# A two-sequence encoder on one core: norm_w applied to the tokens instead of the projection weights, each weight chunk split in one operation per engine

## The chip, the core and the metric

One core of a Trainium2 chip runs the whole program. Its engines are TensorE (PE in the rows, with PEld for its weight loads), VectorE (DVE), ScalarE (ACT), GpSimd (POOL) and SyncE (SP), which issues most transfers. The metric is the device time of one execution in microseconds.

## The reference

A trunk of two layers, D_MODEL 1024, runs over two token sequences, x_prompt of 512 tokens and x_sample of 1024, with the same weights. Cut to what matters:

```
h = rms_norm(x, norm_w[l])            # x * rsqrt(mean(x*x) + EPS) * norm_w
proj = h @ w_in[l]                    # 1024 -> 3328 columns
q, k, v, g_a, u_h, g_h = split(proj)
attn = gqa_attention(rope(rms_norm(q)), rope(rms_norm(k)), v)     # 8 query heads, 2 key heads
o_a = rms_norm(attn, attn_out_norm_w[l]) * silu(g_a)
v_h, x1, x2 = split(short_conv(u_h))
zz = x1 * long_conv(v_h, filter 0);  zz = x2 * long_conv(zz, filter 1)
o_h = rms_norm(zz, hyena_out_norm_w[l]) * silu(g_h)
x = x + concat([o_a, o_h]) @ w_out[l]
...
y = rms_norm(x, final_norm_w)
```

norm_w may be multiplied into h or into the rows of w_in; the product is the same.

## The kernel before

Tokens are handled in tiles of 128 and blocks of 512: block 0 is the short sequence (tiles 0 to 3), blocks 1 and 2 the long one (tiles 4 to 11). Every operand of a large product is kept as two f16 halves, a high one and a low one, and a product is three matmuls (high x high, high x low, low x high). A split into halves is therefore always a pair: ACT writes the high half (a copy with a scale), and DVE writes what is left (scalar_tensor_tensor: in * scale - high).

The weights w_in come in chunks of 256 columns for all 1024 rows, laid out as 128 partitions x 8 row groups x 256 columns (2048 f32 a partition). There are 13 chunks a layer. `w_chunk` (L545) loads one, splits it with eight pairs, one for each row group k, because the scale is norm_w of that group's rows, a column of 128 values (`par_s`, L408 makes it with the factor S_W), and keeps the halves in DRAM for the other sequence; 26 chunks in all are split so. `norm_T` (L484) takes one token tile x with its root r, splits x * r into halves by one pair of 1024 columns, and transposes both halves by a DMA on SP's queue (L492) into hT, the operand of all projections. It is called for four tiles at a time in `first_norm` (L500, layer 0: blocks 1, 2, then 0) and for two tiles at a time in `out` (L1242, layer 1).

Shorthands record nearly every instruction: `act` is L308, `stt` L320, `tt` L328, `ts` L334, `red` L340, `mm` L346, so rows of the profile carry those lines and are told apart by shape.

The work is written as three threads (L45), each a list of parts with a letter, the layer and the sequence (0 short, 1 long): n norm, q queries, keys, values and gates, u convolution inputs and gates, e and f filters, t attention, c long convolutions, a and o the two halves of the output projection. So c10 is the convolution of layer 1 for the short sequence and o11 the last output projection of the long one. `emit` (L353) takes one step at a time from a thread, so that two counters keep a ratio: `dve` grows with every `stt`, `tt` and `red` on DVE (65 + 1.04 per column, L312), `tens` with every matmul (L344). By turns it prefers a part that loads PE or one that loads DVE. A convolution's channel tile c may start only when the part u of its sequence has marked that half as done (L748, L1021). Buffers come from one arena by age. A scheduler then sets each engine's order from the priorities of emission; matmuls of the projections are put 100 places back (PX).

Of the kernel before, what the change touches and what calls it, by code (L numbers as in the profile page):

```python
# [14 lines left out]
ALU = mybir.AluOpType  # L15
# [32 lines left out]
# column offsets of the per-channel parameters  # L48
C_NW, C_CW, C_CB, C_DEC, C_HB, C_AW, C_HW, C_N = 0, 8, 44, 56, 72, 80, 84, 88

S_H = 2.0 ** 10      # normalised activations
S_W = 2.0 ** 8       # projection weights
S_QK = 2.0 ** 7      # q and k after rotation
S_V = 2.0 ** 8
S_P = 2.0 ** 14      # softmax weights
S_C = 2.0 ** 11      # transform matrices
S_F = 2.0 ** 13      # filters
S_OA = 2.0 ** 8      # gated attention output
S_OH = 2.0 ** 10     # gated hyena output
S_U = (2.0 ** 6, 2.0 ** 8)   # folded conv inputs  # L60
S_Y = (2.0 ** 5, 2.0 ** 7)   # spectra of conv outputs
# [11 lines left out]
def _tables():  # L73
# [31 lines left out]
    for L in (LA, LB):  # L105
# [12 lines left out]
        "t_t": np.ascontiguousarray(np.concatenate(ts)[None, :]),  # L118
    }
# [22 lines left out]
class Arena:  # L142
    """On-chip memory in units of 1 KB a partition. A piece is taken that has been free for a while, small
    short-lived ones from the low end and the others from the high end; if there is none, the piece that has
    been free for longest."""
# [41 lines left out]
class Psum:  # L187
    """PSUM banks by class of use; in each class the banks free for longest are taken first."""
# [29 lines left out]
class Thread:  # L218
    """Parts of the work in their order, as steps."""
# [14 lines left out]
class Kern:  # L234
# [24 lines left out]
    def share(self, name, load):  # L259
        """Buffers that several threads read: loaded by the first, freed by the last."""  # L260
        if name not in self.shared:
            self.shared[name] = [load(), 0]
        self.shared[name][1] += 1
        return self.shared[name][0]
# [10 lines left out]
    def keep(self, n):  # L275
        """Columns that stay."""
        o = self.small_n
        self.small_n += n
        assert self.small_n <= 512
        return self.small[:, o:o + n]  # L280

    def tmp(self, n):
        """Columns that are soon used up."""
# [12 lines left out]
    def early(self, ap):  # L296
        """Instructions that free a PSUM bank go before others of their time."""
# [55 lines left out]
    def emit(self, threads):  # L353
        """Emit threads side by side, so that the work of VectorE keeps to RATIO times that of TensorE: by
        turns one whose present part loads TensorE more, or one whose present part loads VectorE more."""
# [31 lines left out]
    def rsqrt(self, out, ss, n, a, b):  # L387
        """out = (a * ss + b) ** -0.5 on [P, n] columns."""
# [11 lines left out]
    def prologue(self):  # L400
# [4 lines left out]
        for l in range(DEPTH):  # L405
            par = self.cols[:, l * C_N:(l + 1) * C_N]
            ps = self.keep(C_N)
            self.ts(ps[:, C_NW:C_NW + 8], par[:, C_NW:C_NW + 8], S_W)  # L408
# [6 lines left out]
            self.par_s.append(ps)  # L415

    def sine(self, out, x, n):
        """out = sin(x) with x taken into [-pi, pi]."""
# [13 lines left out]
    def features(self):  # L432
        """Hidden layers of the filter networks, one layer of the trunk in each half of the partitions;
        each is stored as a stack of a high and a low half."""
# [49 lines left out]
    def norm_T(self, l, x, t, r):  # L484
        m = self.m
        hb = m.alloc(4)
        hl = hb.f16().rearrange("p (h d) -> p h d", h=2)
        self.act(hl[:, 0], x, AF.Copy, scale=r)
        self.stt(hl[:, 1], x, r, hl[:, 0], ALU.mult, ALU.subtract)
# [863 lines left out]
```

## Time and profile before

| | us |
|---|---|
| median of 3 runs | 2420.97 |
| lowest, highest | 2419.26, 2422.30 |
| span of the profiled execution | 2406.2 |
| PE busy | 2061.8 |
| DVE busy | 1853.7 |
| ACT busy | 1146.9 |
| POOL busy | 432.0 |

The span runs from the first to the last instruction of the profiled execution, whose own time outside the span is not listed; the median of the runs is 14.8 us above its span. An engine's busy time is the union of its instructions. Since the engines run side by side, the busy times add up to far more than the span.

### The profile page before, as it was taken

The numbers are of one execution on the slowest core, as the hardware profiler recorded it, in microseconds if no ns is written. First come the engines' busy times: TensorE is split into PE (matmuls) and PEld (weight loads), VectorE is DVE, ScalarE is ACT, GpSimd is POOL, SyncE is SP. The second block draws the span as 40 slices with busy tenths as digits, with TensorE's granted clock in tenths as the row PEclk, the third lists the DMA queues.
The fourth block names the chain that finished last, engine by engine and source line by source line (L and its number), as shares of the span: only waits on it lengthen the run. The fifth ranks groups of instructions, "written<-read, shape, count | busy, mean of one in ns | idle before, by whom it ended". The sixth has DMA issues, their size and how long they took to land. (4 is left out here: it accounts for less than half of the span.)

```text
span 2406.2 us, 39740 instructions
## 1 busy us (share of the span) xinstructions
PE 2061.8 (86%) x15436; PEld 1249.0 (52%) x15436; DVE 1853.7 (77%) x3109; ACT 1146.9 (48%) x2016; POOL 432.0 (18%) x288
## 2 busy tenths in 40 slices
PE   5888889999989889878798778899999998887587
PEld 3656544444554556555575645444446445555453
DVE  7777677777767889976778767687777776998966
ACT  6545445766644234223544445366655652232322
POOL 1323120000110222222223312100011002222321
PEclk9899999999999899989899989999999999999789
DMA  8686659989999668688956678688989999574664
GB/s 230 151 209 174 166 152 216 225 187 203 230 253 265 189 171 215 193 260 266 222 137 191 169 184 215 177 195 192 225 187 197 225 264 305 173 202 118 204 203 136
DMA packets 774534, 485.86 MB, mean 202 GB/s; under 512 B 664838, under 2 KB 720295, under 8 KB 761288
## 3 DMA queue, kind: packets, MB, share of 16 engines
q1 hardware_dynamic: 773952, 482.96, 78.6%
q8 instruction: 121, 1.98, 0.3%
q14 instruction: 69, 0.57, 0.1%
q10 hardware_dynamic: 392, 0.34, 0.1%
HBM read 192.76 MB, written 139.20 MB: 138 GB/s over the span
## 5 line engine op out<-in xcount | busy, mean ns | idle before, releaser
L346 PE MATMUL psum<-arena 128*128 128x512 f16 (+4 forms) x15052 | 2018.5, 300 | 311.7 <-DMA arena<-arena 150.8
L346 PEld LDWEIGHTS <-arena 128*128 128x128 f16 (+2 forms) x15040 | 1199.0, 104 | 1087.5 <-issue 450.4
L328 POOL TENSOR_TENSOR arena<-arena 128x512 f32<-128x512 f32 (+4 forms) x218 | 415.2, 1912 | 1750.7 <-ACT arena L308 1032.4
L328 DVE TENSOR_TENSOR arena<-arena 128x1024 f32<-128x1024 f32 (+4 forms) x484 | 524.5, 1114 | 68.0 <-POOL arena L328 26.9
L308 ACT ACTIVATE arena<-arena 128x512 f16<-128x512 f32 (+4 forms) x359 | 265.1, 753 | 386.3 <-DVE arena L328 208.2
L320 DVE SCALAR_TENSOR_TENSOR arena<-arena,ring 128x1024 f16<-128x1024 f32 (+2 forms) x292 | 352.7, 1224 | 62.7 <-ACT arena L308 61.4
L308 ACT ACTIVATE arena<-psum 128x512 f32<-128x512 f32 (+2 forms) x336 | 177.2, 533 | 386.7 <-PE psum L346 380.6
L308 ACT ACTIVATE arena<-arena,ring 128x1024 f16<-128x1024 f32 (+1 forms) x280 | 287.2, 1044 | 148.9 <-DVE ring L939 29.8
L340 DVE TENSOR_REDUCE ring<-psum 128x1 f32<-128x1024 f32 (+1 forms) x192 | 197.5, 1039 | 55.6 <-PE psum L346 55.4
L308 ACT ACTIVATE arena<-arena,small 128x256 f16<-128x256 f32 (+5 forms) x288 | 167.2, 628 | 143.5 <-DMA arena<-in_p_win_dram 27.0
L320 DVE SCALAR_TENSOR_TENSOR arena<-psum,small,arena 128x511 f32<-128x511 f32 (+2 forms) x240 | 173.4, 743 | 63.8 <-PE psum L346 42.0
L320 DVE SCALAR_TENSOR_TENSOR arena<-psum,arena 128x512 f32<-128x512 f32 (+2 forms) x188 | 107.4, 598 | 129.7 <-ACT arena L308 121.0
L308 ACT ACTIVATE arena<-psum,ring 128x1024 f32<-128x1024 f32 (+1 forms) x192 | 185.6, 967 | 5.0 <-DMA g<-arena 0.5
L320 DVE SCALAR_TENSOR_TENSOR arena<-arena,small 128x256 f16<-128x256 f32 (+1 forms) x224 | 123.5, 583 | 22.9 <-ACT arena L308 15.2
L320 DVE SCALAR_TENSOR_TENSOR arena<-arena 128x512 f32<-128x512 f32 (+5 forms) x135 | 119.4, 890 | 11.7 <-ACT arena L308 11.1
L320 DVE SCALAR_TENSOR_TENSOR arena<-arena,psum 128x512 f32<-128x512 f32 (+1 forms) x144 | 95.6, 679 | 29.4 <-PE psum L346 15.2
L308 ACT ACTIVATE ring<-ring 128x1 f32<-128x1 f32 x192 | 37.4, 197 | 124.7 <-DVE ring L340 124.1
L334 DVE TENSOR_SCALAR ring<-ring 128x1 f32<-128x1 f32 (+8 forms) x339 | 61.1, 184 | 40.5 <-ACT arena L308 37.9
L308 ACT ACTIVATE arena<-psum,small 128x512 f32<-128x512 f32 x72 | 55.3, 771 | 53.7 <-PE psum L346 53.2
L346 PE MATMUL psum<-small,arena 128*128 128x1 f32 x384 | 56.5, 264 | 21.6 <-ACT arena L308 20.3
L346 PEld LDWEIGHTS psum<-small,arena 128*128 128x128 f32 x384 | 56.4, 218 | 33.9 <-ACT arena L308 24.2
L320 DVE SCALAR_TENSOR_TENSOR ring<-ring 128x16 f32<-128x16 f32 (+3 forms) x238 | 45.9, 194 | 5.0
(29 smaller groups left out, 262.9 us busy)
## 6 DMA issues: line engine op xcount, KB each, us to landing
f<-arena SPq DMA_DIRECT2D x128, 256.0 KB, 3.1
arena<-in_p_win_dram SPq DMA_DIRECT2D x26, 1024.0 KB, 6.2
w<-arena SPq DMA_DIRECT2D x26, 1024.0 KB, 4.7
arena<-w SPq DMA_DIRECT2D x26, 1024.0 KB, 6.1
arena<-f SPq DMA_DIRECT2D x16, 1536.0 KB, 7.4
u<-arena SPq DMA_DIRECT2D x24, 512.0 KB, 3.4
arena<-o SPq DMA_DIRECT2D x48, 256.0 KB, 4.2
y<-arena SPq DMA_DIRECT2D x24, 512.0 KB, 5.3
```

The source lines that it names most:

```text
L308: r = self.s.activation(out=out, in_=in_, func=func, scale=scale, **kw)
L320: r = self.v.scalar_tensor_tensor(out=out, in0=a, scalar=sc, in1=b, op0=op0, op1=op1)
L328: r = (eng or self.v).tensor_tensor(out=out, in0=a, in1=b, op=op)
L334: return (eng or self.v).tensor_scalar(out=out, in0=a, scalar1=s1, scalar2=s2, op0=op0, **kw)
L340: r = self.v.tensor_reduce(out=out, in_=in_, op=op, axis=AX, **kw)
L346: return self.pe.matmul(out, lhsT, rhs, start=start, stop=stop)
```

## The change

norm_w moves from the weights to the tokens. `w_chunk` now scales by the constant S_W, so one ACT and one DVE instruction of 2048 columns split a whole chunk. `norm_T` first multiplies the tile by norm_w laid out along the row, on DVE for layer 0's tiles 0 to 7 and on POOL for tiles 8 to 11 and for all of layer 1, into a further 4 KB buffer, and splits that. `norm_rows` makes the row once a layer: eight f32 matmuls of a norm_w column, repeated 128 times by a stride of 0, with a unit matrix (a new input t_eye, loaded on ACT's queue), then one ACT copy of 1024 columns out of PSUM. The row (4 KB a layer) and the unit matrix (1 KB) stay in the arena.

```diff
+        "t_eye": np.eye(P, dtype=np.float32),
...
-            self.ts(ps[:, C_NW:C_NW + 8], par[:, C_NW:C_NW + 8], S_W)
...
+        self.eye = self.m.alloc(1, True).f32(P)
+        self.qs["P"].dma_start(self.eye, self.a["t_eye"])
+        self.nw = [None] * DEPTH
+
+    def norm_rows(self, l):
+        if self.nw[l] is None:
+            p = self.p.alloc("x", 2)
+            for k in range(8):
+                col = V(self.par[l][:, C_NW + k:C_NW + k + 1], 0, [0, P])
+                self.mm(p.ap[:, k * P:(k + 1) * P], col, self.eye, True, True)
+            self.nw[l] = self.m.alloc(4, True)
+            self.act(self.nw[l].f32(D), p.ap, AF.Copy)
+            p.free()
+        return self.nw[l].f32(D)
...
     def norm_T(self, l, x, t, r):
         m = self.m
-        hb = m.alloc(4)
+        hb, nb = m.alloc(4), m.alloc(4)
         hl = hb.f16().rearrange("p (h d) -> p h d", h=2)
-        self.act(hl[:, 0], x, AF.Copy, scale=r)
-        self.stt(hl[:, 1], x, r, hl[:, 0], ALU.mult, ALU.subtract)
+        xn = nb.f32(D)
+        self.tt(xn, x, self.norm_rows(l), ALU.mult, eng=self.v if l == 0 and t < 8 else self.g)
+        self.act(hl[:, 0], xn, AF.Copy, scale=r)
+        self.stt(hl[:, 1], xn, r, hl[:, 0], ALU.mult, ALU.subtract)
+        nb.free()
...
         W = m.alloc(8)
-        r = raw.f32(2048).rearrange("p (k c) -> p k c", k=8)
         w = W.f16().rearrange("p (h k c) -> p h k c", h=2, k=8)
-        for k in range(8):
-            nw = self.par_s[l][:, C_NW + k:C_NW + k + 1]
-            self.act(w[:, 0, k], r[:, k], AF.Copy, scale=nw)
-            self.stt(w[:, 1, k], r[:, k], nw, w[:, 0, k], ALU.mult, ALU.subtract)
+        hl = W.f16().rearrange("p (h n) -> p h n", h=2)
+        self.act(hl[:, 0], raw.f32(2048), AF.Copy, scale=S_W)
+        self.stt(hl[:, 1], raw.f32(2048), S_W, hl[:, 0], ALU.mult, ALU.subtract)
         raw.free()
```

The rest of the diff takes out comments. Since the planner's two counters change (a split chunk counts 2195 instead of 2648, a product on DVE 1130), the order of emission changes as well. Three places of the built program show it. In the rows, arena is the one on-chip buffer, ring and small hold columns, psum_64 is PSUM.

DVE at the start. In the order before, the pieces of the first chunk (128x256) and the square root's columns (ring) stand ahead of the four splits of the first token block (128x1024):

```order
L334 TENSOR_SCALAR arena_63<-psum_64,small_65 128x512
L320 SCALAR_TENSOR_TENSOR ring_66<-ring_66 128x4
L320 SCALAR_TENSOR_TENSOR arena_63<-arena_63 128x512
L334 TENSOR_SCALAR arena_63<-psum_64,small_65 128x512
L320 SCALAR_TENSOR_TENSOR ring_66<-ring_66 128x4
L320 SCALAR_TENSOR_TENSOR arena_63<-arena_63,small_65 128x256
L334 TENSOR_SCALAR arena_63<-arena_63 128x512
L320 SCALAR_TENSOR_TENSOR arena_63<-arena_63,small_65 128x256
L334 TENSOR_SCALAR arena_63<-arena_63 128x512 x2
L320 SCALAR_TENSOR_TENSOR arena_63<-arena_63,ring_66 128x1024 x4
L320 SCALAR_TENSOR_TENSOR arena_63<-arena_63 128x512
```

In the new order the same place holds four products (TENSOR_TENSOR 128x1024; the last two are shown) and one split of 128x2048:

```order
L329 TENSOR_TENSOR arena_63<-arena_63 128x1024
L335 TENSOR_SCALAR ring_66<-ring_66 128x4
L329 TENSOR_TENSOR arena_63<-arena_63 128x1024
L329 TENSOR_TENSOR ring_66<-ring_66 128x4
L321 SCALAR_TENSOR_TENSOR arena_63<-arena_63 128x2048
L321 SCALAR_TENSOR_TENSOR ring_66<-ring_66 128x4
L335 TENSOR_SCALAR arena_63<-psum_64,small_65 128x512
L321 SCALAR_TENSOR_TENSOR ring_66<-ring_66 128x4
L335 TENSOR_SCALAR arena_63<-psum_64,small_65 128x512
```

The products stand ahead of the root's columns; the four splits of the tokens follow only from the 42nd row on.

POOL at the start, before: the two products are those of the rotation table.

```order
L793 MEMSET arena_63 128x1
L328 ISA
L328 TENSOR_TENSOR arena_63<-arena_63 128x1024 x2
L793 MEMSET arena_63 128x1 x2
L328 TENSOR_TENSOR arena_63<-arena_63 128x512
```

The same place after:

```order
L329 ISA
L329 TENSOR_TENSOR arena_63<-arena_63 128x1024 x3
L809 MEMSET arena_63 128x1
L329 TENSOR_TENSOR arena_63<-arena_63 128x1024 x3
L809 MEMSET arena_63 128x1
L329 TENSOR_TENSOR arena_63<-arena_63 128x512
```

Six products of 1024 columns stand where two stood; four are those of tiles 8 to 11.

SP at the end of the program, before. L1065 is the transpose of a convolution's operand, L1000 the store of its gated result, L1266 a load of the residual, L1283 a store of the output (out_1 long, out_0 short sequence), L1209 a load for the last projection:

```order
L1266 DMA arena_63<-y1_11_18457 128x1024
L1257 DMA arena_63<-in_final_norm_w_dram 128x1024
L1065 DMA_TRANSPOSE arena_63<-arena_63 128x8x128
L1266 DMA arena_63<-y1_3_18720 128x1024
L1283 DMA out_1_dram<-arena_63 128x1024 x2
L1000 DMA o1_14708<-arena_63 128x4x128 x2
L1266 DMA arena_63<-y1_2_18579 128x1024
L1000 DMA o1_14708<-arena_63 128x4x128 x2
L1283 DMA out_1_dram<-arena_63 128x1024 x2
L1209 DMA arena_63<-o1_14708 128x2x512 x4
L1283 DMA out_1_dram<-arena_63 128x1024 x2
L1283 DMA out_0_dram<-arena_63 128x1024 x4
```

And after, where the lines are 16 higher (L1081, L1016, L1282, L1299, L1225), L1205 loads weights of w_out kept in DRAM and L1108 a filter:

```order
L1282 DMA arena_63<-y1_3_20138 128x1024
L1282 DMA arena_63<-y1_2_20011 128x1024
L1299 DMA out_1_dram<-arena_63 128x1024 x2
L1282 DMA arena_63<-y1_1_19971 128x1024
L1108 DMA arena_63<-f1_1_3_13827 128x1024
L1205 DMA arena_63<-wo1_1_20094 128x2048 x2
L1081 DMA_TRANSPOSE arena_63<-arena_63 128x8x128
L1205 DMA arena_63<-wo1_1_20094 128x2048
L1081 DMA_TRANSPOSE arena_63<-arena_63 128x8x128
L1016 DMA o1_14363<-arena_63 128x4x128 x4
L1225 DMA arena_63<-o1_14363 128x2x512 x4
L1299 DMA out_0_dram<-arena_63 128x1024 x4
```

Before, six stores of out_1 stand behind the last transpose; after, none does: they stand ahead of both last transposes, and w_out's rows are loaded again for the short sequence. The loads of u1_2 and u1_3, with which these two channel tiles begin, stand 54 and 61 rows behind the last store of the projections (g1_7), where they stood 10 ahead of it and 12 behind.

## Rows read from the trace of the kernel before

**Rows 1.** The page: span, then busy us, share and instructions by engine.
```profile
span 2406.2 us, 39740 instructions
...
PE 2061.8 (86%) x15436; PEld 1249.0 (52%) x15436; DVE 1853.7 (77%) x3109; ACT 1146.9 (48%) x2016; POOL 432.0 (18%) x288
```

**Rows 2.** Windows: stretch, its us, busy us (instructions) by engine, PEclk, DMA share, GB/s.
```profile
2000.00:2300.00 300.00, 235.50 (x2034) 168.58 (x2035) 265.99 (x279) 86.53 (x133) 85.91 (x33) 0.89 0.65 200
2319.20:2406.20 87.00, 70.25 (x447) 39.24 (x445) 60.81 (x136) 22.80 (x39) 11.59 (x7) 0.95 0.47 158
0.00:34.60 34.60, 13.98 (x31) 5.77 (x31) 25.87 (x64) 21.80 (x36) 6.39 (x10) 1.00 0.80 236
```

**Rows 3.** Waits: engine and line, for whom: us in total, times, longest.
```profile
PE psum L346 <- DMA arena<-arena: 150.8, 73, 8.1
...
PE psum L346 <- ACT arena L308: 99.5, 44, 10.8
```

**Rows 4.** The page: chain that ended last, shares of the span by engine.
```profile
PE 17%; DVE 13%; DMA 7%; issue 2%; ACT 1%; POOL 0%; SPq 0%; DVEq 0%; ACTq 0%; POOLq 0%
```

**Rows 5.** Groups by form: count, busy us, mean ns, idle before and what ended it.
```profile
L328 DVE TENSOR_TENSOR arena<-arena 128x1024 f32<-128x1024 f32 x232 | 316.7, 1388 | 45.8 <-POOL arena L328 18.8 <-DMA arena<-f 17.4 <-ACT arena L308 6.3
L320 DVE SCALAR_TENSOR_TENSOR arena<-arena,ring 128x1024 f16<-128x1024 f32 x216 | 288.2, 1349 | 54.2 <-ACT arena L308 53.3
L308 ACT ACTIVATE arena<-arena,ring 128x1024 f16<-128x1024 f32 x216 | 242.8, 1141 | 114.8 <-DVE ring L819 21.5 <-POOL arena L328 20.1 <-DVE ring L320 19.6
...
L328 POOL TENSOR_TENSOR arena<-arena 128x1024 f32<-128x1024 f32 x52 | 154.4, 2981 | 429.2 <-ACT arena L308 122.1 <-DMA arena<-f 80.8 <-DVE arena L328 59.3
...
L320 DVE SCALAR_TENSOR_TENSOR arena<-arena,small 128x256 f16<-128x256 f32 x208 | 102.1, 525 | 15.6 <-ACT arena L308 7.9 <-DMA f<-arena 5.7 <-issue 1.9
L308 ACT ACTIVATE arena<-arena,small 128x256 f16<-128x256 f32 x208 | 90.5, 496 | 31.6 <-DMA arena<-in_p_win_dram 27.0 <-DMA f<-arena 2.3 <-PE psum L346 1.7
...
L346 PE MATMUL psum<-arena 128*128 128x512 f32 x6 | 5.1, 954 | 12.2 <-ACT arena L308 12.2
```

**Rows 6.** Groups by form, DVE alone, 38 to 46 us.
```profile
L320 DVE SCALAR_TENSOR_TENSOR arena<-arena,ring 128x1024 f16<-128x1024 f32 x4 | 4.9, 1276 | 0.0
...
L320 DVE SCALAR_TENSOR_TENSOR arena<-arena,small 128x256 f16<-128x256 f32 x2 | 0.9, 474 | 0.0
```

**Rows 7.** Timeline of the start: start us, us, engine, instruction, count, idle before.
```profile
21.00 5.63 POOL L328 TENSOR_TENSOR arena<-arena 128x1024 f32<-128x1024 f32 x2 [9.68 <-DMA arena<-in_q_norm_w_dram]
21.06 9.05 DVE L320 SCALAR_TENSOR_TENSOR arena<-arena,ring 128x1024 f16<-128x1024 f32 x4
...
34.68 9.22 PE L346 MATMUL psum<-arena 128*128 128x256 f16 x77 [1.37 <-DMA arena<-arena]
...
39.76 4.86 DVE L320 SCALAR_TENSOR_TENSOR arena<-arena,ring 128x1024 f16<-128x1024 f32 x4
```

**Rows 8.** Timeline of the end: last operand transpose, stores of its result.
```profile
2344.86 1.90 SPq L1065 DMA_TRANSPOSE arena<-arena  x1
...
2366.10 1.59 SPq L1000 DMA_DIRECT2D o<-arena  x2
```

**Rows 9.** Groups by form, PE alone, 2290 to 2406.2 us.
```profile
L346 PE MATMUL psum<-arena 128*128 128x512 f16 x288 | 65.5, 386 | 0.2 <-DMA arena<-o 0.2
L346 PE MATMUL psum<-arena 128*128 128x256 f16 x120 | 15.2, 276 | 5.7 <-DVE arena L328 3.2 <-ACT arena L308 2.5
L346 PE MATMUL psum<-arena 128*128 128x128 f16 x144 | 11.6, 249 | 2.5 <-DMA arena<-arena 2.1 <-DVE small L328 0.3
```

**Rows 10.** Groups by form, DVE alone, 2319.2 to 2406.2 us.
```profile
L320 DVE SCALAR_TENSOR_TENSOR arena<-arena,ring 128x1024 f32<-128x1024 f32 x12 | 15.0, 1282 | 0.2
...
L320 DVE SCALAR_TENSOR_TENSOR ring<-ring 128x2 f32<-128x2 f32 x36 | 5.8, 160 | 1.0
L320 DVE SCALAR_TENSOR_TENSOR arena<-arena 128x512 f32<-128x512 f32 x7 | 5.2, 738 | 0.1
```

## The prediction

> **What bounds the kernel now.** I read the totals of the page first: TensorE (PE) is busy 2061.8 of 2406.2 us, VectorE (DVE) 1853.7, ScalarE (ACT) 1146.9, GpSimd (POOL) 432.0 [rows 1]. So PE sets the pace, and 344 us of the span are stretches in which it stands. The windows show where [rows 2]: in the first 34.6 us it works 14.0 us; from 2000 to 2300 us it works 235.5 of 300 while DVE works 266.0, so there DVE leads; in the last 87 us it works 70.3. The waits say for whom PE stands: 150.8 us for transfers inside the arena (the transposes), 99.5 us for ACT [rows 3]. The chain that ended last covers only the last part of the span, and of that DVE is 13 of the 37 hundredths that PE, DVE and transfers hold between them [rows 4]: about a third of a microsecond taken off DVE there reaches the end. The median of the runs, 2420.97, is 14.8 us above the profiled span, which I take as fixed; the sum is made against the span and carried to the median.
>
> **The splits of the weights.** Each of 26 fresh chunks loses eight pairs of 256 columns and gets one pair of 2048. On DVE 208 pieces take 102.1 us [rows 5]. An undisturbed piece takes 474 ns and an undisturbed split of 1024 columns 1276 ns [rows 6], which is 1.04 ns a column over a fixed part, so 2048 columns take about 2.34 us and 26 of them 61 us: 41 us less. On ACT 208 pieces take 90.5 us; from 496 ns for 256 and 1141 ns for 1024 [rows 5], 2048 take 2.0 us and 26 of them 52 us: 38 us less. ACT is half idle, so I count this at nothing; the cover is that idle half. A whole chunk is ready some 4 us after its load, where the first of eight pieces was ready after 1 us, but matmuls of the projections stand behind everything else of their time and PE has that other work; without that cover it would be up to 3 us a chunk.
>
> **The multiplications by norm_w.** Eight tiles on DVE and sixteen on POOL, each 128x1024 in f32. On DVE one takes 1.39 us in the mean of the whole run, and, when nothing is in its way, no more than the 1276 ns of the split [rows 5, 6]: 8 of them 10 us. On POOL one takes 2981 ns [rows 5]: 48 us, of which POOL has plenty. But the two disturb each other. At 21.00 us POOL multiplies two tiles in 5.63 us, and the four DVE splits beside them take 9.05 us; the same four take 4.86 at 39.76 with POOL quiet [rows 7]. So one microsecond of POOL cost DVE 0.75 there. Over the whole run the rate is far lower: 216 splits and 232 products of that size lie 73 and 112 ns above 1276 [rows 5, 6], together 42 us for 432 us of POOL [rows 1], 0.1, and the other sizes can add as much again. For 48 us of new POOL work the bounds are 5 and 36 us of DVE; I take 12, a quarter, nearer to the whole run's rate, since in the pair at 21.00 us every DVE instruction met POOL. DVE in all: -41 + 10 + 12 = -19 us, of which a third, 6, reaches the end (bounds 0 and 19).
>
> The Trainium skill ("SBUF — State Buffer", Who interferes with whom) says that a DVE instruction with two SBUF inputs and a POOL instruction that reads SBUF hold their shared read port in turn, and that the later one waits in full. The pair of rows at 21 and 39.76 us agrees with that; by it all 48 us would be lost if every POOL product met such an instruction, and DVE would gain 48 + 10 - 41 = 17 us of work instead of losing 19. That is the last rival below.
>
> **norm_w in rows.** Eight f32 matmuls of 128x128 and one copy out of PSUM for each layer. A 128x512 f32 matmul takes 954 ns [rows 5], so I take a quarter of it, 0.24 us: 2 us a layer. In layer 0 PE stands anyway; in layer 1 it is work in PE's row. +2 us with its copy (0 to 4).
>
> **The start.** Before, PE first runs densely at 34.68 us [rows 7], when the four splits of the first block, done by about 30 us, have been transposed. Now DVE's first tiles stand behind four products (4 x 1.28, 5.1 us) and one 2.34 us split instead of six pieces of 0.47 that stood ahead: +4.6 us. The new order puts six products on POOL there instead of two, so POOL is in DVE's way for up to 18 us instead of 5.6, at 0.75 up to 9 us more. Against that, the second block's products no longer need DVE, and its transposes follow the first's at once. Bounds 0 and 13; I take +6.
>
> **Layer 1's norm.** The product of a tile on POOL (3 us) runs beside the square and the root, which need the same tile; but POOL takes its work in order, and the hand-over of a pair is two products, 6 us, against two squares at 1.14 and a dozen narrow DVE steps at 0.16 [rows 5, 10], 4.2 us. +2 us (0 to 8, when a convolution's product is queued ahead).
>
> **The order of everything else.** The emission planner counts DVE and PE work, and the change moves both counts, so from the second block on the threads interleave differently. Most of that is of no fixed sign, but at the end of the program it is plain. In the old order the last convolution of the short sequence stands among the output tiles of the long one: six of its eight stores (out_1) come after the last fold's transpose. In the new order all eight are out before it, and the wo1_1 rows are loaded a second time; two channel tiles (c10, channels 2 and 3) have both their convolutions after the last matmul of the long sequence's output. What PE has from that point, by the new order's count, is 192 matmuls of 128x128, 96 of 128x256, 12 narrow ones and 96 of 128x512. At 81, 127 and 227 ns of busy time each [rows 9] that is 15.6 + 12.2 + 2 + 21.8 = 52 us. How long it takes: one convolution, from the transpose of its operand (2344.86) to the store of its result (2366.10), took 21.2 us; from there to the end 40.1 us [rows 8]. Two convolutions in series, 48 matmuls (3.9 us) for sharing with the second channel tile, and the end: 21.2 + 21.2 + 3.9 + 40.1 = 86.4 us. In its last 87 us the old kernel got 70.3 us of PE work done [rows 2], the new one would get 52. So about 19 us of PE work lie ahead of that point that used to lie behind it: **+19 us** (bounds +5, if output tiles slip in after all, and +35, if the two tiles do not overlap).
>
> The same holds for DVE: behind that point stand 15 instructions of 1024 columns at 1.28 us, 14 of 512 at 0.74, 12 of 256 at about 0.4 (an estimate between its neighbours) and 38 narrow ones at 0.16 [rows 10], 40 us, where the last 87 us held 60.8 [rows 2].
>
> **The stretch before the end.** In exchange, the short sequence's attention and projections now run on beside the long convolution, where DVE led. From 2000 to 2300 us PE stood 64.5 us and DVE 34 [rows 2]. With PE work always at hand no more than DVE's 34 can be won, and 20 us more DVE work now have to go in there. I take -10 (bounds 0 and -34).
>
> **The sum.** +6 - 6 + 2 + 2 + 19 - 10 = +13 us: 2420.97 + 13 = **2434 us**. It rests on the tail: without it the change would be a small gain.
>
> **The rivals.**
> 1. The stretch and DVE win. For it: DVE is the engine that PE shares its idle time with late in the run [rows 2, 4], and the change takes work from it everywhere. Against: most splits stand in the first half, where PE is fed. Start +3, rows and norm +4, DVE -10, stretch -34, tail +19: -18, 2403 us.
> 2. The order gives back what the tail takes: stretch -20 instead of -10, start +3: 0, 2421 us.
> 3. POOL blocks DVE. One mechanism: DVE's two-input instructions wait out each of the sixteen POOL products, in the start and while layer 1's tokens are normed. It decides from about 36 us of wait on, three quarters of the 48. Then DVE gains 17 us of work, a third of it shows (+6 instead of -6), the start costs 13: +13 + 12 + 7 = +32, 2453 us.
> 4. The change not doing what it says (the large splits cut up again or the products all on DVE) is ruled out by the new order, which shows one ACT and one DVE instruction of 128x2048 a chunk.
>
> **How the numbers follow.** Forecast 0.50, own range 2424 to 2452; rival 1 0.31; rival 2 0.12; rival 3 0.07. About 0.2%, 5 us, is what a measurement of this kernel can tell from no change. The first and the third are slower but for a small part of the first's range, which gives 0.55 slower with 0.13 same and 0.32 faster. For 8 in 10 the range goes down past rival 1's value, to 2397, and up past rival 3's, to 2458.
>
> **What would show it.** In the profile after: DVE's busy time about 20 us lower, ACT's about 36 lower, POOL's 48 higher; 26 splits of 128x2048 at 2.3 us; the first dense PE work at 38 to 43 us; in the last 87 us PE busy near 52 instead of 70, with waits for transposes and ACT between two bursts of 128x128 matmuls. If the last 87 us hold 65 us or more of PE work, the tail is not exposed and the forecast falls; if DVE is not lower at all, rival 3 holds; if PE's idle time between 1900 and the tail is far below the old one, rival 1.

## Result: 2513 us, slower by 3.9%, and the profile after

The changed kernel takes **2513.48 us** (median of 4 runs, 2509.48 to 2515.82), the kernel before 2420.11 beside it: ratio **1.039, interval 1.037 to 1.041**. Forecast were 2434 us, 2397 to 2458. The sign was right, the size was not: +93 instead of +13. The page of the profiled execution, against [rows 1]:

```profile
span 2507.7 us, 39509 instructions
...
PE 2100.1 (84%) x15468; PEld 1262.2 (50%) x15468; DVE 1869.7 (75%) x2933; ACT 1120.0 (45%) x1838; POOL 459.8 (18%) x304
```

The span grew by 101.5 us, 8 more than the median: the execution of the kernel before that was traced is shorter than nearly all others of that kernel (see "The missing link" below). PE's idle time (span less busy) went from 344.4 to 407.6, +63; its busy time grew by 38, of which the norm rows are 6. DVE is 16 us *up*, where about 20 down was forecast; ACT 27 down, POOL 28 up.

The forms that the change touches, against [rows 5] (count, busy us, mean ns, idle before). First DVE:

```profile
L329 DVE TENSOR_TENSOR arena<-arena 128x1024 f32<-128x1024 f32 x240 | 325.7, 1372 | 51.6 <-POOL arena L329 15.7 <-DMA arena<-f 15.2 <-ACT arena L309 13.1
...
L321 DVE SCALAR_TENSOR_TENSOR arena<-arena 128x2048 f16<-128x2048 f32 x26 | 60.6, 2330 | 38.0 <-ACT arena L309 37.9
```

Then POOL, whose group was 154.4 us for 52:

```profile
L329 POOL TENSOR_TENSOR arena<-arena 128x1024 f32<-128x1024 f32 x68 | 187.6, 2767 | 514.4 <-DMA arena<-f 165.2 <-DVE arena L321 66.8 <-issue 63.9
```

Then ACT's splits, and PE's norm rows:

```profile
L309 ACT ACTIVATE arena<-arena 128x2048 f16<-128x2048 f32 x26 | 49.6, 1906 | 38.8 <-DMA arena<-in_p_win_dram 21.3 <-DMA f<-arena 9.6 <-DMA arena<-arena 4.9
```

```profile
L347 PE MATMUL psum<-arena,small 128*128 128x128 f32 x32 | 5.9, 339 | 7.3 <-DMA arena<-in_t_eye_dram 7.2
```

The splits came out as costed: 2330 ns on DVE (2.34 us forecast), 1906 on ACT (2.0), 41.5 and 41 us less in all. So the loss is elsewhere. (The 16 f32 matmuls of the norm rows stand as 32 instructions.)

**Where it is.** I cut both traces where PE has done the same share of its work (7.5, 35, 55, 85 and 100% of the columns of its matmuls, counted from the instructions' shapes, those with 64 output rows at half and f32 at four times), so that a stretch can be compared though the order differs. Windows: stretch, its us, busy us (instructions) of PE, PEld, DVE, ACT, POOL, PEclk, DMA share, GB/s. The kernel before:

```profile
0.00:208.40 208.40, 156.90 (x1345) 110.89 (x1346) 161.72 (x334) 114.96 (x186) 48.49 (x46) 0.92 0.76 189
208.40:841.00 632.60, 572.42 (x3965) 315.36 (x3963) 467.80 (x810) 342.17 (x617) 80.66 (x61) 0.95 0.87 209
841.00:1331.00 490.00, 409.79 (x3399) 282.66 (x3398) 397.78 (x621) 202.00 (x348) 119.39 (x69) 0.93 0.76 206
1331.00:2014.00 683.00, 614.53 (x4263) 331.46 (x4261) 494.48 (x931) 376.21 (x691) 84.01 (x72) 0.97 0.85 205
2014.00:2406.20 392.20, 308.19 (x2476) 208.60 (x2474) 331.91 (x416) 111.53 (x175) 99.45 (x40) 0.90 0.60 187
```

The changed kernel:

```profile
0.00:225.80 225.80, 159.60 (x1334) 114.83 (x1335) 169.16 (x294) 113.85 (x161) 61.30 (x51) 0.83 0.71 175
225.80:861.40 635.60, 570.12 (x3982) 309.31 (x3980) 467.20 (x756) 329.21 (x548) 80.61 (x59) 0.95 0.86 206
861.40:1376.30 514.90, 423.18 (x3402) 285.79 (x3400) 412.81 (x604) 201.29 (x330) 136.86 (x78) 0.90 0.74 198
1376.30:2095.40 719.10, 626.19 (x4363) 347.93 (x4360) 499.99 (x823) 348.96 (x580) 102.71 (x76) 0.94 0.81 197
2095.40:2507.70 412.30, 321.00 (x2401) 204.38 (x2399) 320.56 (x459) 126.72 (x220) 78.36 (x40) 0.89 0.65 191
```

Stage by stage the loss is 17, 3, 25, 36 and 20 us. The first is the start, the last holds the exposed end. But 61 of the 101 lie in the third and fourth, which hold layer 1's norms (transposes of `norm_T` from 1102 to 1452 us before, 1127 to 1559 after), and for which the sum had next to nothing. No one wait grew to that size: PE's largest even fell, against [rows 3]:

```profile
PE psum L347 <- DMA arena<-arena: 136.5, 69, 8.6
PE psum L347 <- ACT arena L309: 114.3, 45, 11.3
PE psum L347 <- DVE arena L321: 59.0, 31, 8.2
```

### The profile page after: what moved, and what is told of

Read it like the earlier page. It is cut to its first block, busy times and chain, and to the rows that moved or that the text cites. A ratio compares the mean times of both kernels' runs of the same rounds, so it can differ in the third digit from the quotient of the medians.

```text
span 2507.7 us, 39509 instructions
## 1 busy us (share of the span) xinstructions
PE 2100.1 (84%) x15468; PEld 1262.2 (50%) x15468; DVE 1869.7 (75%) x2933; ACT 1120.0 (45%) x1838; POOL 459.8 (18%) x304
## 5 line engine op out<-in xcount | busy, mean ns | idle before, releaser
L347 PE MATMUL psum<-arena 128*128 128x512 f16 (+4 forms) x15052 | 2052.8, 302 | 362.5 <-DMA arena<-arena 136.5
L329 POOL TENSOR_TENSOR arena<-arena 128x512 f32<-128x512 f32 (+4 forms) x234 | 440.7, 1890 | 1907.1 <-ACT arena L309 1004.1
L329 DVE TENSOR_TENSOR arena<-arena 128x1024 f32<-128x1024 f32 (+4 forms) x492 | 536.7, 1115 | 92.5 <-POOL arena L329 30.0
L309 ACT ACTIVATE arena<-arena 128x512 f16<-128x512 f32 (+5 forms) x385 | 313.8, 830 | 449.4 <-DVE arena L321 204.3
L309 ACT ACTIVATE arena<-psum 128x512 f32<-128x512 f32 (+3 forms) x338 | 180.0, 538 | 371.6 <-PE psum L347 366.4
L321 DVE SCALAR_TENSOR_TENSOR arena<-psum,small,arena 128x511 f32<-128x511 f32 (+2 forms) x240 | 173.7, 744 | 99.5 <-PE psum L347 71.2
L321 DVE SCALAR_TENSOR_TENSOR arena<-arena 128x512 f32<-128x512 f32 (+6 forms) x161 | 179.5, 1123 | 46.3 <-ACT arena L309 44.9
L309 ACT ACTIVATE arena<-arena,small 128x512 f32<-128x512 f32 (+4 forms) x80 | 77.2, 971 | 80.2 <-DVE arena L321 13.3
L321 DVE SCALAR_TENSOR_TENSOR ring<-ring 128x16 f32<-128x16 f32 (+3 forms) x238 | 51.8, 218 | 6.4
L329 DVE TENSOR_TENSOR ring<-ring 128x16 f32<-128x16 f32 (+4 forms) x155 | 48.7, 315 | 6.2 <-ACT arena L309 3.0
```

The costliest lines, as they stand in the source:

```text
L309: r = self.s.activation(out=out, in_=in_, func=func, scale=scale, **kw)
L321: r = self.v.scalar_tensor_tensor(out=out, in0=a, scalar=sc, in1=b, op0=op0, op1=op1)
L329: r = (eng or self.v).tensor_tensor(out=out, in0=a, in1=b, op=op)
L347: return self.pe.matmul(out, lhsT, rhs, start=start, stop=stop)
```

## The experiments

Two theories at first: **A**, the new emission order makes the loss; **B**, the new operations do. The planner's counters can be fed either way, so order and operations can be crossed. All runs are compared with the kernel before on the same chip, with 95% intervals.

**1. The changed kernel in the old order.**

```
-    self.mm(p.ap[...], col, self.eye, True, True)
+    self.pe.matmul(p.ap[...], col, self.eye, start=True, stop=True)   # not counted
...
-    self.tt(xn, x, self.norm_rows(l), ALU.mult, eng=...)
+    (...).tensor_tensor(out=xn, in0=x, in1=self.norm_rows(l), op=ALU.mult)
...
+    self.dve += 7 * 65                     # a chunk counts as eight pieces
...
-    tight = self.m.n - sum(self.m.used) < ROOM
+    tight = self.m.n - sum(self.m.used) + self.extra < ROOM
```

> The changed kernel, whole, but with the planner's counters fed as in the kernel before: a split chunk counts 8 x 331, the norm products and the norm_rows matmuls count nothing, the arena's 9 KB are added back where the planner asks for room. All 2529 emission steps then come in the order of the kernel before. Theory A (most of the +93 us comes from the order that the changed counters give, in the middle and in the tail): 2400 to 2435 us, the last part of the trace like the one of before. Theory B (the added and merged operations themselves cost it: POOL's products, 2.3 us operations in front of narrow ones): 2480 to 2520 us, and DVE's idle and busy time as after the change.

Measured: 2499.56 us, 1.032 (1.028 to 1.036). Theory A falls as the main cause: with every emission step in the old place, 78 of the 93 us stay. The time lies in theory B's range, but DVE's busy time doesn't stay up as B said: 1856.1 us, 2.4 over the kernel before.

**2. The kernel before in the new order.** The reverse edit on the counters, no other.

> The kernel before with nothing of the change but its counters: a split chunk counts 2195, 8 norm tiles count 1130 each, the norm_rows matmuls 430, and 9 KB are taken from the planner's room. All 2529 emission steps come in the order of the changed kernel, the instructions are those of before. Theory A (order): 2480 to 2515 us, with poor stretches of TensorE at the places where the changed kernel has them and an exposed tail. Theory B (operations): 2410 to 2440 us.

Measured: 2473.34 us, 1.021 (1.017 to 1.024). That lies between the two ranges. The order alone costs the old instructions 51 us, yet taking it away gave the changed kernel only 14. The two don't add up. The end is as in the changed kernel: its last 87 us (columns as above)

```profile
2384.60:2471.60 87.00, 49.20 (x304) 30.62 (x304) 48.19 (x91) 16.58 (x27) 11.29 (x8) 0.77 0.31 107
```

**3. The splits alone**, old order.

```
-    for k in range(8):  act(w[:, 0, k], r[:, k], scale=nw); stt(w[:, 1, k], r[:, k], nw, ...)
...
+    act(hl[:, 0], raw.f32(2048), scale=S_W); stt(hl[:, 1], raw.f32(2048), S_W, ...)
+    self.dve += 7 * 65
```

> Only the split of a chunk in one operation per engine, by S_W; norm_w is left out of the computation altogether; the counters stay those of before, so the emission order is that of before. Theory A (order does it): 2395 to 2420 us, DVE busy about 41 us and ACT about 40 us lower. Theory B (operations): a merged 2.3 us split in front of narrow operations costs as much as it saves, 2420 to 2450 us.

Measured: 2405.39 us, 0.994 (0.992 to 0.996): 17 us faster. DVE's busy time fell by 26 us (1853.7 to 1827.8), not by the 41 that the splits alone lose, and ACT's by 35.

**4. The tokens' half alone**, old order, eight-piece splits by a constant.

> Only the other half: norm_w on the tokens (norm_rows, nb tiles, products on DVE and POOL), chunks split in eight pieces by S_W; counters and emission order of before. Theory A (order does it): 2415 to 2440 us, by the start's 6 us and POOL's blocking. Theory B (operations): 2460 to 2510 us, most of the loss is here, with DVE's waits for POOL.

Measured: 2510.75 us, 1.037 (1.033 to 1.041), just above theory B's range. So nearly all of the loss is in this half, +89 us in the old order. Its third stage takes 534.7 us, 45 more than before:

```profile
862.10:1396.80 534.70, 432.67 (x3394) 288.36 (x3393) 435.04 (x634) 200.45 (x351) 141.78 (x82) 0.88 0.67 186
```

What is in this half: products on POOL, 9 KB that stay in the arena (and 4 KB in each norm_T), norm rows (with two PSUM banks for a moment, so that later PSUM banks can fall differently, which no run takes apart), a longer start. Theory **P** says the products, theory **M** the memory.

**5. The memory alone.** The kernel before, no added instruction, that only holds the space; by its allocations every buffer of the arena lies as in experiment 4.

```
+    self.m.alloc(1, True)                      # in prologue
...
-    hb = m.alloc(4)
+    hb, nb = m.alloc(4), m.alloc(4)            # in norm_T; nb freed at its end
+    if l not in self.nw: m.alloc(4, True)      # once a layer
...
```

> The kernel before with no instruction of the change, in its own emission order, that only holds what the norm half of the change holds of the arena (1 KB for the eye, 4 KB for each layer's norm rows, for good, and 4 KB in each norm_T while it lasts), so every buffer lies where it lies in the norm-only kernel. Theory M (memory: with 9 of 202 KB gone, buffers come free later and transfers and splits wait for them): 2470 to 2510 us, nearly all of the norm half's +89. Theory P (the products themselves, on POOL and in front of the transposes): within 10 us of the kernel before.

Measured: 2469.47 us, 1.021 (1.018 to 1.024): +48 us, just under theory M's range and about half of the +89, not nearly all of it. PE, DVE, ACT and POOL have no new instruction; the 64 more of the page are semaphore waits. Its page and its five stages:

```profile
span 2466.9 us, 39804 instructions
...
PE 2092.0 (85%) x15436; PEld 1257.0 (51%) x15436; DVE 1855.9 (75%) x3109; ACT 1149.5 (47%) x2016; POOL 422.5 (17%) x288
```

```profile
0.00:211.80 211.80, 157.96 (x1350) 113.91 (x1351) 162.47 (x334) 116.57 (x187) 49.78 (x46) 0.90 0.73 187
211.80:842.30 630.50, 570.39 (x3959) 311.28 (x3957) 455.05 (x799) 342.17 (x616) 76.14 (x61) 0.95 0.88 209
842.30:1365.60 523.30, 422.94 (x3402) 284.86 (x3401) 419.83 (x645) 204.87 (x353) 116.24 (x74) 0.90 0.71 194
1365.60:2055.20 689.60, 620.79 (x4258) 333.14 (x4257) 485.44 (x918) 372.87 (x685) 80.27 (x69) 0.96 0.85 202
2055.20:2466.90 411.70, 319.91 (x2476) 213.76 (x2474) 333.14 (x415) 112.99 (x175) 100.07 (x40) 0.86 0.59 179
```

The first two stages are even with the kernel before; the third is 33 us longer and the last 20, and both are where the changed kernel loses too. The 30 us that PE stands longer are spread over its three largest waits; before [rows 3] they were 150.8, 99.5 and, not shown there, the third:

```profile
PE psum L346 <- DVE arena L320: 35.7, 21, 7.9
```

With the memory held:

```profile
PE psum L346 <- DMA arena<-arena: 166.2, 77, 9.1
PE psum L346 <- ACT arena L308: 107.6, 45, 8.4
PE psum L346 <- DVE arena L320: 45.0, 23, 9.4
```

**6. The products, all on DVE** (experiment 4 with `self.v` for every tile).

> The norm-only kernel of the last experiments (2510 us, emission order of before) with all 24 products on DVE and none on POOL. Theory P (POOL's products block DVE, or come late for the transposes): 2425 to 2460 us. Theory M (memory): 2495 to 2520 us, since 16 products of 1.2 us on DVE change little.

Measured: 2487.47 us, 1.029 (1.025 to 1.032): 23 us back of 89, between the ranges of P and M. DVE's busy time fell although it has sixteen more products; the pages of experiment 4 and of this one:

```profile
PE 2105.1 (84%) x15468; PEld 1261.0 (50%) x15468; DVE 1892.5 (75%) x3115; ACT 1133.7 (45%) x2018; POOL 473.1 (19%) x304
```

```profile
PE 2089.8 (84%) x15468; PEld 1255.4 (50%) x15468; DVE 1878.0 (76%) x3131; ACT 1136.0 (46%) x2020; POOL 432.4 (17%) x288
```

Sixteen products of 1.23 us (as they run on DVE in experiment 15) are 20 us, so without them DVE stands at 1858: POOL's products had cost DVE 34 us. That is rough: DVE's busy time also moves by 14 us, 1853.7 to 1867.7, with the places alone (the kernel before and experiments 8, 10, 11).

**7. The rows given back.** Experiment 4, with the eye freed after use and a layer's rows after its twelfth tile.

```
...
+    self.left[l] -= 1
+    if self.left[l] == 0: self.nw[l].free()
...
```

> The norm-only kernel, products where they were, but the eye is freed right after the norm_rows matmuls (and loaded again for layer 1) and a layer's norm rows after its twelfth tile, so that between the first norms and layer 1's norms, and after those, the arena has its 202 KB again. Theory M: 2420 to 2460 us, with the loss in the stretch of layer 1's norms alone. Theory P: 2495 to 2520 us.

Measured: 2475.57 us, 1.023 (1.020 to 1.026): 35 of the 89 us back, more than the products gave, but not down to 2460.

**8, 10, 11. Other places, nothing else.** `AGE = 8e4` becomes 5e4, 3e4, 12e4 in the kernel before.

> The kernel before, same instructions and emission order, with one constant of its arena changed (a buffer counts as old after 5e4 of the planner's ns and not 8e4), which gives other places to the same buffers without taking memory. A measure of what chance in the placement alone does. Theory M, that room is what counts: within 15 us of 2420. If it moves by 30 us or more, any change to the allocations moves the time by as much, and neither memory nor the products can be named as the cause by single runs.

> The kernel before with the arena's age constant at 3e4, nothing else: another draw of places without taking memory. The draw at 5e4 gave 2429 (+8). If room is what costs, 2410 to 2435; if places alone, by chance, make +48, draws like this one will scatter over 2410 to 2470.

> The kernel before with the arena's age constant at 12e4: a third draw of places without taking memory. Room: 2410 to 2435. Chance in the places: anywhere in 2410 to 2470.

Measured: 2429.46 us, 1.0045 (1.0022 to 1.0067); 2412.64, 0.9975 (0.9955 to 0.9995); 2449.03, 1.012 (1.009 to 1.015). Four draws of places with the same instructions and the same emission order lie between 2413 and 2449, 36 us apart. The expectation for room, up to 2435, was passed by the third. Experiment 8's expectation had named 30 us as the size from which single runs can't tell memory from products; so the prices of 14 to 35 us here, each from one draw, can be chance in part. The third stage alone, 33 us longer in experiment 5, takes about 490, 501, 514 and 519 us in these four draws (before, 10, 11, 8). A draw is more than addresses: the framework's scheduler sets each engine's order from the dependences it sees, and a place that is used again makes a dependence. These two weren't taken apart.

**12. The memory held, in another draw** (experiment 5 at 3e4).

> The kernel before that holds 1 + 4 + 4 KB for good and 4 KB in each norm_T (2469 us, +48), with the arena's age constant at 3e4: a second draw of places with the memory taken. Room: 2455 to 2480 again. Chance in the places: as likely 2420 to 2450.

Measured: 2446.49 us, 1.011 (1.008 to 1.015). Against the same constant without the memory (2412.64) that is +34, where the first pair gave +48. But the time lies in the range expected for chance (2420 to 2450), not in the one for room, and within the four draws without the memory. Held, the two draws are 2446 and 2469; not held, 2413 to 2449. So it is likely that the held memory costs time, but how much of the +34 and +48 is room and how much another draw isn't shown.

**9, 17. The split in a form that keeps norm_w on the weights**: ACT scales the raw chunk in place.

```
+    for k in range(8): self.act(r[:, k], r[:, k], AF.Copy, scale=<norm_w column>)
+    self.act(hl[:, 0], raw.f32(2048), AF.Copy)
+    self.tt(hl[:, 1], raw.f32(2048), hl[:, 0], ALU.subtract)
```

> Norm_w stays on the weights, but ACT alone applies it: eight 256-wide ACT operations scale the raw chunk in place, then one 2048-wide ACT copy makes the high half and one 2048-wide DVE subtraction the low half (no norm rows, no nb, no products on tokens; emission order and memory of before). DVE loses 182 operations and about 41 us of busy time as in the split-only kernel (2405 us, -16.6), ACT gains about 26 x 1.9 us. If the split's gain is DVE's time, 2400 to 2415 us; if the later high half (some 2 us more per chunk on ACT) is waited for by TensorE, 2415 to 2430.

> ACT scales the raw chunk by norm_w in place, one split per engine, and the arena's age constant at 3e4 (the draw that gave the kernel before 2412.6 us, ratio 0.9975). If the two add up (2425.7 - 2420.6 = +5 for the split's form, -8 for the draw): 2412 to 2422 us. If every edit draws anew, within 2400 to 2450.

Measured: 2425.66 us, 1.0026 (1.0007 to 1.0045), and 2432.62, 1.0059 (1.0038 to 1.0080). DVE is as low as with the splits alone, 26 us under the kernel before; pages of 9 and of 3:

```profile
PE 2077.9 (85%) x15436; PEld 1256.5 (52%) x15436; DVE 1827.6 (75%) x2927; ACT 1189.9 (49%) x2040; POOL 430.5 (18%) x288
```

```profile
PE 2065.8 (86%) x15436; PEld 1250.6 (52%) x15436; DVE 1827.8 (76%) x2927; ACT 1111.9 (46%) x1832; POOL 436.1 (18%) x288
```

and yet there is no gain. Either ACT's 43 us more are waited for, or the 17 us of experiment 3 were partly a lucky draw. PE's waits for ACT speak for the first: 99.5 us before [rows 3], less in experiment 3 and not in 9 (3 ahead of 9):

```profile
PE psum L346 <- ACT arena L308: 81.4, 36, 9.8
PE psum L346 <- ACT arena L308: 97.2, 43, 9.7
```

By these the split's gain may have come through ACT, whose 38 us the prediction counted at nothing; with one draw each it isn't shown. The edits didn't add up either: 3e4 was the better draw for the kernel before and the worse one here.

**13, 14. The changed kernel in other draws** (2e4 and 6e4).

> The changed kernel with the arena's age constant at 2e4, its own order: another draw of places. If the loss is of the change, 2485 to 2525 us; if it was an unlucky draw, 2440 to 2480.

> The changed kernel with the arena's age constant at 6e4: a third draw. If the loss is of the change, 2485 to 2525 us; an unlucky draw, 2440 to 2480.

Measured: 2565.51 us, 1.060 (1.057 to 1.063), and 2556.53, 1.056 (1.053 to 1.059), both above what was expected. The changed kernel's draws are 2513, 2557 and 2566, the kernel before's 2413 to 2449: they don't overlap. So the loss is the change's and not one unlucky draw; the one that was timed is the best of three. (These two constants weren't tried on the kernel before.)

**15. The products off POOL, in the new order.**

> The changed kernel with all 24 products on DVE, not counted by the planner, so in its own emission order and places. If POOL's products cost what they cost in the order of before (23 us): 2485 to 2495 us, and the narrow DVE operations at 15 to 31 us back at 0.15 us each. If they cost only where they ran beside the start's chain: 2500 to 2510.

Measured: 2503.17 us, 1.034 (1.031 to 1.038): 10 us back, less than the 23 of the old order. That is the value expected if the products cost only at the start, but the first stage shortened by 2 us alone (223.8) and the third by 10 (504.6, from 514.9), where eight of layer 1's twelve tiles are normed. It is so in the old order too, where moving them shortened the third stage from 534.7 to 517.3. Both differences are below the 30 us by which that stage varies among the draws of the kernel before, so the place of the cost is likely, not shown.

**16, 18. All three mended**: old order, products on DVE, rows given back (18 at 3e4).

> The whole change with three things mended: emission order of before, products on DVE, eye and norm rows given back to the arena after their last use. By adding up the single runs: 2421 + 89 - 23 - 35 - 17 = 2435 us, 2425 to 2450. If chance in the places is larger than these prices, anywhere up to 2480.

> The mended change (emission order of before, products on DVE, eye and rows given back) with the age constant at 3e4: a second draw. By the prices 2435 us; if 2466 was an unlucky draw, 2425 to 2450; if something of the change is still unpriced, 2455 to 2480.

Measured: 2466.00 us, 1.018 (1.015 to 1.021), and 2447.04, 1.011 (1.009 to 1.013). The prices were each measured against another kernel and don't add up: 2435 was the sum. The first lies where chance was expected, the second where 2466 would be an unlucky draw. Over the kernel before at the same constants +47 and +34 stay, with the split's gain inside, so the three together take away half to two thirds of the +93. Most of what stays lies in the third stage (experiment 16; the same columns), 36 us longer than before, while the first is only 3.5 longer:

```profile
0.00:211.90 211.90, 153.80 (x1304) 110.26 (x1305) 163.06 (x299) 110.35 (x158) 50.05 (x45) 0.92 0.71 184
842.30:1368.30 526.00, 430.55 (x3374) 290.34 (x3373) 416.63 (x610) 198.77 (x320) 119.39 (x69) 0.88 0.69 189
```

There layer 1's norm rows are in the arena even in this kernel, and twelve products more are on DVE, which has 417 us of work there for 398. Which of the two, or the draw, is open.

No version with the change in it beats the kernel before. The only kernel here that does and computes the same is experiment 10, by 0.25%, from one constant.

## Why the prediction missed, step by step

**The splits: right.** -41 us on DVE was forecast and 41.5 measured (102.1 to 60.6). "About a third reaches the end" gave -14, and experiment 3 measured -17; but experiments 9 and 17, with the same 26 us off DVE's total, gained nothing. The third isn't a rule, and that -14 and -17 agree is luck: the -14 was worked out from 41 us, and DVE as a whole lost 26.

**POOL against DVE: mis-sized.** I took 12 us of DVE between 5 and 36. Experiments 4 and 6 give 34; in the new order, experiment 15 (DVE 1871.9 with 20 us of products added, against 1869.7) gives 18, both within the bounds and both rough (experiments 8, 10 and 11 move DVE by up to 14 us with no product). In time it was 23 and 10 us, where a third of 12 was counted, 4. DVE's forecast -19 became +16 in the changed kernel and +2 in the old order (experiment 1), so order and places have a part in that as well.

**The start: the moment right, the cost larger.** First dense PE work at 38 to 43 us was forecast; it came at 41.56, and +6 (0 to 13) was the term. The first stage lost 17.4, more than the upper bound, of which experiment 5 puts 3 on the memory. POOL was in the way as the step feared (start us, us, instruction; against [rows 7]):

```profile
14.57 10.76 POOL L329 TENSOR_TENSOR arena<-arena 128x1024 f32<-128x1024 f32 x3 [13.62 <-DMA arena<-in_x_sample_dram]
15.25 2.32 DVE L335 TENSOR_SCALAR ring<-ring 128x4 int32<-128x4 int32 x1
17.48 1.21 DVE L329 TENSOR_TENSOR arena<-arena 128x1024 f32<-128x1024 f32 x1
18.62 2.31 DVE L329 TENSOR_TENSOR ring<-ring 128x4 f32<-128x4 f32 x1
20.85 2.28 DVE L321 SCALAR_TENSOR_TENSOR arena<-arena 128x2048 f16<-128x2048 f32 x1
23.05 2.29 DVE L321 SCALAR_TENSOR_TENSOR ring<-ring 128x4 f32<-128x4 f32 x1
25.33 2.33 POOL L329 TENSOR_TENSOR arena<-arena 128x1024 f32<-128x1024 f32 x1
```

Moving the products off POOL alone doesn't mend it (experiment 15, first stage 223.8 us), nor does it in the old order with the memory held (219.9 in experiment 6, from 224.2 in experiment 4); with the rows given back and the large splits too it is 211.9 (experiment 16), 3.5 over before. The order alone makes it 214 (experiment 2), and the places alone move it between 208 and 215. So the term was too small, and what each part takes of the 17 isn't shown.

**The end: the work right, its price not shown.** PE's last 87 us, 70.3 before [rows 2], were forecast at 52. The changed kernel:

```profile
2420.70:2507.70 87.00, 49.04 (x304) 30.61 (x304) 48.07 (x91) 16.19 (x26) 10.61 (x8) 0.79 0.32 103
```

49.0, and 49.2 in experiment 2, which has nothing of the change but the order. The stretch ahead of it gained too. The changed kernel ends 101 us later, so the same microseconds don't hold the same work; the 419.2 us ahead of the last 87 can be compared, first before, then after:

```profile
1900.00:2319.20 419.20, 345.01 (x2678) 221.27 (x2677) 351.50 (x456) 146.99 (x274) 96.35 (x42) 0.92 0.75 213
2001.50:2420.70 419.20, 353.20 (x2659) 219.21 (x2657) 335.56 (x441) 135.78 (x244) 82.73 (x40) 0.92 0.74 214
```

PE stands 66 us there instead of 74: 8 gained, 10 forecast. So reading the order's end told 21 us of exposed work and a gain ahead of it, as said. What they are worth in time no run measures alone: the last stage is 20 us longer in the changed kernel, but also in experiment 5, which has the old order.

**The step that failed** is the one on the order of everything else. Its sentence "Most of that is of no fixed sign" put the middle of the program at nothing, and with it the arena was left out: nowhere does the sum ask what 9 KB for good and 4 KB in passing do to the places of all other buffers. In their place the runs showed +51 us from the order alone, with the old instructions (experiment 2), which is beyond all four draws of the kernel before; +48 and +34 from the memory without a new instruction on any compute engine (5 and 12), the second within those draws; and -35 on giving the rows back (7). "No fixed sign" is not the same as nothing: three redraws of the kernel before gave -8, +8 and +28. The kernel before was the second best of its four draws, and two of three redraws cost time. The norm half, +17 in the sum (start 6, rows and norm 4, a third of 10 + 12), measured +89. How much of that is room, how much chance in the places and which wait carries it stays open.

**The missing link from idle to clock.** The sum took a microsecond of PE's standing for a microsecond of time, and the 14.8 us between span and median for fixed. The second is wrong: in every run that lists both, an execution lasts 1.7 to 2.1 us longer than its span. 63 other executions of the kernel before span 2405.0 to 2429.0 us (median 2419.0) at mean granted clocks of 0.928 to 0.941 (median 0.934); the traced one, 2406.2 at 0.940, is shorter than all but one. So a difference of spans against this trace overstates a loss by up to 13 us. The first is too little: in experiment 5 PE stands 30.5 us longer (344.4 to 374.9), and the same 15436 matmuls take 30.2 us longer at a clock of 0.922. Of the +48 between the medians that leaves some 18 us for slower matmuls (an estimate, 48 less 30.5), and all four executions of experiment 5, 0.922 to 0.924, were granted less than any of the kernel before. In the changed kernel the +93 are 63 of idle time, 6 for the norm rows and some 24 of slower matmuls (the same estimate).

The rivals: rival 1 fell, since ahead of the tail 8 us came back and not 34, and rival 2, which needs 20 there, fell with it. Rival 3's sign showed (DVE not lower at all, +16 where it had +17), but its mechanism, measured by itself, took 34 and 18 us of DVE, less than the 36 from which it was to decide, and 2453 left 60 us unexplained. None had the memory.

## What to carry to other kernels

Where one planner sets the order and one allocator the places, first ask of an edit what it keeps in memory and what it tells the planner, and only then what its instructions cost: here holding 13 KB moved the time by 34 and 48 us, taking the products off POOL by 10 and 23, the 26 large splits by 17, all but the 48 within the scatter of the places. Before believing a gain or loss of a per cent, measure the scatter of the kernel itself by a constant that changes places alone (here 36 us), and give the forecast a range at least so wide, leaning to the slow side when the kernel at hand is a good draw. And cross the two halves of a change with its order by faking the planner's counts: experiments 1 to 4 show so which half costs.

## What the hardware showed that I had not expected

A DVE operation of four columns, 0.15 us in experiment 15, takes 2.3 us beside POOL's 128x1024 f32 product, and one after another: in the rows of the start above three narrow ones each wait out a whole product, while the wide DVE operations between them run at their own 1.21 and 2.28 us, and POOL waits for those (10.76 us for three products, one of which takes 2.33 at 25.33 us). So in these rows POOL's cost to DVE goes by the count of meetings, not by the columns that DVE moves. The same start with the products on DVE:

```profile
16.71 0.15 DVE L329 TENSOR_TENSOR ring<-ring 128x4 f32<-128x4 f32 x1
16.78 1.22 DVE L506 TENSOR_TENSOR arena<-arena 128x1024 f32<-128x1024 f32 x1
17.92 0.15 DVE L321 SCALAR_TENSOR_TENSOR ring<-ring 128x4 f32<-128x4 f32 x1
```

The Trainium skill ("SBUF — State Buffer", Who interferes with whom) says that the later of the two fully blocks for the whole instruction. For the two-input operations these rows agree. That the integer operation with one input waits as well (15.25 us) the Trainium skill, in the same section, has only for modes in which DVE uses both ports; no run here tells its mode.

And PE's busy time isn't a property of the instructions alone. The same 15436 matmuls took 2061.8 us in the trace of the kernel before and 2085.1 in experiment 8's (span 2429.0), which differs in places alone; PE stood 344.4 and 343.9 us. The mean granted clock was 0.940 and 0.929. This need not be the places' doing: experiment 8's ten executions were granted 0.929 to 0.940, the kernel before's 0.928 to 0.941, so one execution of one program can differ from another by as much.
